# Cosine-similarity attention on one core: four late warm-up dummies behind the first transposes, with new instruction orders

## The chip, the cores and the metric

The kernel runs on one core of a Trainium2 chip. Its engines work in parallel, each through its own queue in program order: TensorE (PE, matmuls and transposes), ScalarE (ACT, exponentials), VectorE (DVE), GpSimd (POOL) and SyncE (SP), which issues nearly all DMAs. They wait for one another on semaphores. The metric is the device time of one launch in microseconds; lower is better.

## What is computed

Queries, keys and values have the shape 8 x 12 x 512 x 64 in float32 (96 heads, 512 rows of 64 numbers), and tau is 0.1.

```
Q_norm = Q / (np.linalg.norm(Q, axis=-1, keepdims=True) + 1e-10)
K_norm = K / (np.linalg.norm(K, axis=-1, keepdims=True) + 1e-10)
scores = np.einsum('bhqd,bhkd->bhqk', Q_norm, K_norm) / tau
weights = np.exp(scores - np.max(scores, axis=-1, keepdims=True))
weights = weights / (np.sum(weights, axis=-1, keepdims=True) + 1e-10)
return np.einsum('bhqk,bhkd->bhqd', weights, V).astype(np.float32)
```

A score is at most 10 in size, so the kernel leaves out the subtraction of the maximum.

## The kernel before

**Tiling.** The work is cut into 48 pairs of heads, s = 0 to 47. For each pair the kernel issues the same small operations, and each has a name of the form `KIND.s.part`:

- `LD.s.0` and `LD.s.1` load queries and keys (256 KB each, line 429, into one of 18 buffers); `LV.s` loads the values (line 432, one of 6).
- `SQ.s` squares both (line 250, mostly on GpSimd). `SSQ.s` adds squares by eight matmuls with an identity (line 268) and `RED.s` (VectorE, line 276) finishes the sums.
- The norms follow. For the first three pairs they are a logarithm and an exponential on ScalarE (`LN.s`, line 282, `EX.s.w`, line 286). For the later ones VectorE iterates in steps `NEW.g.k` (lines 390 to 402) for a group of one or two pairs.
- `SCL.s.0` (queries, VectorE) and `SCL.s.1` (keys, mostly GpSimd) scale the rows into bf16 (line 296).
- `TR.s` transposes the scaled rows on TensorE (line 484) and `EVA.s` copies them from PSUM (VectorE, line 490). Every sixth pair from 9 on transposes its keys by a DMA instead (`XT.s.1`).
- `SCO.s.c`, c = 0 to 3, computes the scores of 128 keys against 512 queries for both heads (two matmuls, line 512), and `EXP.s.c` takes their exponential on ScalarE, 128 x 1024 numbers in one instruction (line 527). The scores lie in PSUM in two halves (`scps`), so TensorE can be at most two chunks ahead of ScalarE.
- `VC.s` converts the values to bf16 (GpSimd, line 532). `PV.s.h.t` multiplies weights and values (four matmuls, line 543); a column of ones in the values gives the sum. `RCP.s` and `NRM.s` (VectorE, lines 557 and 559) divide, and `ST.s` stores (SP).

**The head of the program.** Pair 0 is cut by heads to start sooner. Its loads are four halves. `SQ.0.w.h` (w = 0 queries, 1 keys; h is the head) runs on ScalarE, only `SQ.0.0.1` on GpSimd. `RED.0.w.h` (line 318), `LN.0.h`, `EX.0.h`, `SCL.0.w.h` (line 327), the four transposes of `TR.0.w.h` (line 333), the copy `EVA.0.w.h` (line 338), `SCO.0.h.c` (line 359) and `EXP.0.h.i` (line 364) follow. The transposes need the identity that `one` and `eye` (lines 224 and 225) write on GpSimd; `vone` writes the columns of ones. Pair 1 has its own transposes and copies (lines 301 and 349).

**Dummies.** `warm.0` to `warm.18` are matmuls of 256 columns on a zeroed tile, whose results nothing reads (line 237). `fill.k` are dummies of the same kind that the order puts later. `FILL = (9, 2)` counts those that write the scores' bank and those that write an output bank: in the order of before, fill.0 to fill.7 stand right behind warm.18, fill.8 behind the first two transposes, and fill.9 and fill.10 among the scores of pair 1.

**Order.** Each engine's order is a list written out by hand (`ORDER`). An instruction waits on semaphores for what it needs, and a queue does not pass an instruction that waits. Buffers in PSUM are taken in the order of the list: `x`, `o0` and `o1` are banks that the square sums, the transposes and the outputs share. For TensorE the order of before begins so:

```
warm.15 warm.16 warm.17 warm.18 fill.0 fill.1 fill.2 fill.3 fill.4 fill.5 fill.6 fill.7 TR.0.1.0 TR.0.0.0
fill.8 SCO.0.0.0 SCO.0.0.1 TR.0.1.1 TR.0.0.1 SCO.0.0.2 SCO.0.0.3 SSQ.1 SCO.0.1.0 SCO.0.1.1 SCO.0.1.2 SCO.0.1.3
```

Of the kernel before, what the change touches and what calls it, by code (L numbers as in the profile page):

```python
# [124 lines left out]
def bass_cosine_similarity_attention_kernel(  # L125
# [515 lines left out]
XT = {9: (1,), 15: (1,), 21: (1,), 27: (1,), 33: (1,), 39: (1,), 45: (1,)}  # L641
# [3 lines left out]
WARM = 19  # L645
FILL = (9, 2)
# [5 lines left out]
LOGS = 3  # L652
# [32 lines left out]
        NRM.1 RED.7.0 NEW.2.3 NEW.2.4 NEW.3.0 EVA.4 NEW.2.5 NEW.3.1 NEW.2.6 NEW.3.2 SCL.5.0 NEW.2.7 RCP.2 NRM.2
        RED.9.0 NEW.3.3 NEW.3.4 EVA.5 NEW.3.5 NEW.3.6 NEW.3.7 SCL.6.0 RCP.3 NRM.3 RED.8.0 SCL.7.0 EVA.6 NEW.4.0
        NEW.4.1 RCP.4 NRM.4 NEW.4.2 NEW.4.3 NEW.4.4 EVA.7 NEW.4.5 NEW.4.7 RCP.5 NRM.5 NEW.4.6 RED.10.0 SCL.8.0 SCL.9.0
        EVA.8 EVA.9 RED.11.0 NEW.5.0 NEW.5.1 RCP.6 NRM.6 NEW.5.2 NEW.5.3 NEW.5.4 NEW.5.5 RED.13.0 NEW.5.7 NEW.5.6
        SCL.10.0 RCP.7 NRM.7 RED.12.0 SCL.11.0 EVA.10 NEW.6.0 NEW.6.1 NEW.6.2 EVA.11 NEW.6.3 NEW.6.4 NEW.6.5 NEW.6.6
        SCL.12.0 RED.15.0 RCP.8 NEW.6.7 NRM.8 RED.14.0 NEW.7.0 SCL.13.0 EVA.12 NEW.7.1 NEW.7.2 NEW.7.3 RCP.9 NRM.9  # L690
        NEW.7.4 NEW.7.5 RED.16.0 NEW.7.6 SCL.14.0 EVA.13 NEW.7.7 RCP.10 NRM.10 RED.17.0 EVA.14 SCL.15.0 NEW.8.0
        NEW.8.1 NEW.8.2 EVA.15 NEW.8.3 NEW.8.4 NEW.8.5 RCP.11 NEW.8.6 NRM.11 NEW.8.7 SCL.17.0 RED.18.0 SCL.16.0 RCP.12
        NRM.12 RED.19.0 NEW.9.0 NEW.9.1 NEW.9.2 NEW.9.3 NEW.9.4 EVA.16 RCP.13 NRM.13 RED.20.0 NEW.9.5 EVA.17 NEW.9.7
        NEW.9.6 SCL.18.0 RCP.14 NRM.14 RED.21.0 SCL.19.0 NEW.10.0 EVA.18 EVA.19 NEW.10.1 NEW.10.2 RCP.15 NRM.15
# [15 lines left out]
        RCP.37 NRM.37 NEW.21.3 NEW.21.4 NEW.21.5 RED.44.0 EVA.41 NEW.21.6 SCL.42.0 NEW.21.7 SCL.43.0 RCP.38 NRM.38  # L710
        RED.45.0 EVA.42 NEW.22.0 RCP.39 NRM.39 NEW.22.1 RED.46.0 NEW.22.2 NEW.22.3 EVA.43 NEW.22.4 NEW.22.5 RCP.40
        NRM.40 NEW.22.6 NEW.22.7 RED.47.0 SCL.44.0 RCP.41 NRM.41 SCL.45.0 NEW.23.0 EVA.44 NEW.23.1 NEW.23.2 RCP.42
        NEW.23.3 NRM.42 NEW.23.4 EVA.45 NEW.23.5 NEW.23.6 SCL.46.0 NEW.23.7 RCP.43 NRM.43 EVA.46 SCL.47.0 RCP.44
        NRM.44 EVA.47 RCP.45 NRM.45 RCP.46 NRM.46 RCP.47.0 NRM.47.0 RCP.47.2 RCP.47.1 NRM.47.2 NRM.47.1""",
    "pe": """
# [113 lines left out]
```

## Time and profile before

| | |
|---|---|
| median of three runs | 192.68 us (192.48 to 192.89) |
| profiled execution | 194.2 us, its span 192.4 us |
| ScalarE busy | 182.2 us, 95% |
| TensorE busy | 173.6 us, 90% |
| GpSimd busy | 160.8 us, 84% |
| VectorE busy | 145.1 us, 75% |
| read and written | 37.75 MB and 12.58 MB |

The span runs from the first instruction to the last; the profiled execution's own time has the launch around it. Busy times do not count waiting. In a timeline row the first number is the start in microseconds, the second the time from the first start to the last end of the merged instructions; then come engine, line, operation, what is written and read, and the count. In brackets stands the engine's idle time before the row and what released it. In a row of waits stand the total, the number of times and the longest. Instructions of one engine overlap at their ends by about 0.1 us. In a row of windows the engine's busy time stands behind the length, and behind the count in brackets stand the granted TensorE clock, the DMA share and GB/s.

### The profile page before, as it was taken

To read this page: it belongs to the slowest core of one execution; us is meant where nothing else is said; L and a number is where in the kernel's file an instruction comes from. 1 tells how busy PE (TensorE), PEld (TensorE's weight loads), DVE (VectorE), ACT (ScalarE), POOL (GpSimd) and SP (SyncE) were. 2 spreads that over 40 slices of the span, in tenths; PEclk is the share of its full clock that TensorE was granted. 3 is DMA by queue.
4 is the path that set the end of the run, shared out by engine and by line. 5 is a ranking of instruction groups with operands and counts; after the bars stand their busy time and mean duration, and the time that the engine had idled before them with its cause. 6 is when DMAs were issued, how large, how long until landed. Compare 5 with 4: busy or idle time off the path is not lost.

```text
span 192.4 us, 7254 instructions
## 1 busy us (share of the span) xinstructions
PE 173.6 (90%) x3030; PEld 111.3 (58%) x3030; DVE 145.1 (75%) x451; ACT 182.2 (95%) x209; POOL 160.8 (84%) x147
## 2 busy tenths in 40 slices
PE   7989899998999997898989898999999989997893
PEld 5546566655665665566556565656665656664542
DVE  2789987869878866868868868678689778677523
ACT  5489999999999999999999999999999999999992
POOL 4399599999999997999999999999899997353400
PEclk9999999999999999999999999999999999999998
DMA  5999999479998899989999999999999686513135
GB/s 159 355 349 351 361 342 355 152 241 342 371 334 193 242 345 356 307 214 333 357 332 254 342 298 298 362 237 316 307 385 328 149 259 194 162 27 113 58 114 163
DMA packets 56257, 51.73 MB, mean 269 GB/s; under 512 B 6944, under 2 KB 56224, under 8 KB 56224
## 3 DMA queue, kind: packets, MB, share of 16 engines
q1 hardware_dynamic: 55792, 50.93, 85.0%
q8 instruction: 24, 0.39, 0.8%
q10 hardware_dynamic: 432, 0.33, 0.5%
q14 instruction: 9, 0.07, 0.1%
HBM read 37.75 MB, written 12.58 MB: 262 GB/s over the span
## 4 chain that ended last, share of the span: by engine, by line
ACT 56%; POOL 19%; PE 13%; DMA 4%; DVE 3%; issue 2%; SPq 1%; DVEq 0%; POOLq 0%
ACT et L527 53%; POOL sq L250 11%; POOL qn L296 6%; DMA qk<-in_K_dram 4%; PE scps L512 3%; PE bps L543 3%; PE scps L237 3%; POOL vb L532 2%; ACT et L364 1%; PE bps L268 1%; DVE qn L296 1%; PE bps L484 1%; DVE qt L490 1%; SPq L429 1%; PE scps L359 1%
## 5 line engine op out<-in xcount | busy, mean ns | idle before, releaser
L527 ACT ACTIVATE et<-scps 128x1024 bf16<-128x1024 f32 x184 | 169.9, 1053 | 1.3 <-PE scps L512 1.1
L250 POOL TENSOR_TENSOR sq<-qk 128x1024 bf16<-128x1024 f32 (+2 forms) x48 | 87.9, 1842 | 5.3 <-DMA qk<-in_Q_dram 5.0
L512 PE MATMUL scps<-qt 64*128 64x512 bf16 x376 | 73.7, 385 | 8.1 <-ACT et L527 7.2
L543 PE MATMUL bps<-vb,et 128*128 128x65 bf16 x1504 | 67.4, 194 | 1.9 <-DVE ob L559 0.6
L543 PEld LDWEIGHTS bps<-vb,et 128*128 128x128 bf16 x1504 | 53.0, 98 | 25.0 <-issue 15.3
L296 POOL TENSOR_TENSOR qn<-qk,rk 128x512 bf16<-128x512 f32 x44 | 45.3, 1044 | 12.1 <-DVE rk L398 5.9
L490 DVE COPY qt<-bps 128x1024 bf16<-128x1024 bf16 (+1 forms) x46 | 29.8, 649 | 12.7 <-PE bps L484 12.4
L296 DVE TENSOR_TENSOR qn<-qk,nps 128x512 bf16<-128x512 f32 x50 | 33.5, 682 | 1.1 <-ACT nps L286 0.6
L559 DVE TENSOR_TENSOR ob<-bps,rd 128x512 f32<-128x512 f32 x47 | 32.5, 691 | 1.5 <-DMA out_dram<-ob 0.2
L512 PEld LDWEIGHTS scps<-qt 64*128 64x128 bf16 x376 | 18.3, 93 | 24.7 <-ACT et L527 12.9
L532 POOL TENSOR_SCALAR vb<-vf 128x512 bf16<-128x512 f32 x48 | 29.5, 628 | 1.0 <-DMA vf<-in_V_dram 1.0
L268 PE MATMUL bps<-sq,ident 128*128 128x128 bf16 x376 | 29.1, 220 | 0.3 <-POOL sq L250 0.3
L268 PEld LDWEIGHTS bps<-sq,ident 128*128 128x128 bf16 x376 | 21.2, 98 | 10.2 <-issue 7.1
L557 DVE RECIPROCAL rd<-bps 128x8 f32<-128x8 f32 x47 | 9.7, 207 | 19.1 <-PE bps L543 18.8
L484 PE MATMUL bps<-ident,qn 64*128 64x64 bf16 x680 | 17.8, 191 | 3.4 <-DVE nps L276 0.8
L484 PEld LDWEIGHTS bps<-ident,qn 64*128 64x128 bf16 x680 | 13.7, 95 | 11.3 <-DVE nps L276 2.6
L276 DVE TENSOR_REDUCE nps<-bps 128x16 f32<-128x128 f32 x45 | 13.2, 294 | 1.8 <-PE bps L268 1.8
L394 DVE SCALAR_TENSOR_TENSOR nps<-nps,ys 128x32 f32<-128x32 f32 (+1 forms) x48 | 9.3, 194 | 1.0
L390 DVE TENSOR_TENSOR nps<-nps,ys 128x32 f32<-128x32 f32 (+1 forms) x48 | 9.2, 192 | 0.9
L237 PE MATMUL scps<-warm_in 128*128 128x256 bf16 x28 | 6.1, 409 | 1.1 <-DVE warm_in L232 1.1
L237 PEld LDWEIGHTS scps<-warm_in 128*128 128x128 bf16 x28 | 4.0, 146 | 2.7 <-DVE warm_in L232 1.1
L364 ACT ACTIVATE et<-scps 128x1024 bf16<-128x1024 f32 (+1 forms) x5 | 4.0, 846 | 1.4 <-PE scps L359 1.4
(45 smaller groups left out, 46.0 us busy)
## 6 DMA issues: line engine op xcount, KB each, us to landing
vf<-in_V_dram SPq DMA_DIRECT2D x48, 256.0 KB, 5.9
qk<-in_Q_dram SPq DMA_DIRECT2D x47, 256.0 KB, 5.8
qk<-in_K_dram SPq DMA_DIRECT2D x47, 256.0 KB, 5.7
out_dram<-ob SPq DMA_DIRECT2D x47, 256.0 KB, 4.7
qk<-in_Q_dram SPq DMA_DIRECT2D x2, 128.0 KB, 2.7
qk<-in_K_dram ACTq DMA_DIRECT2D x2, 128.0 KB, 2.9
out_dram<-ob SPq DMA_DIRECT2D x1, 128.0 KB, 2.5
qt<-qn SPq DMA_TRANSPOSE x7, 3.6
```

The lines of the kernel that those rows point to most:

```text
L237: P.add(key, "pe", needs, lambda e: e.matmul(out=bank[:, 0:256], lhsT=warm_in[:, 0:128], rhs=warm_in[:, :], start=True, stop=True))
L250: emit = lambda e: e.tensor_tensor(out=b, in0=a, in1=a, op=ALU.mult)
L268: last = e.matmul(out=ps[:, 0:128], lhsT=ident[:, :], rhs=sq[s % R_SQ][:, :, 8 * k : 8 * k + 8], start=(k == 0), stop=(k == 7))
L276: lambda e: e.tensor_reduce(out=dst(None), in_=ps[:, 0:128].rearrange("p (w g e) -> p w g e", w=2, e=8), axis=AX.X, op=ALU.add))
L296: lambda e: e.tensor_tensor(out=o, in0=x, in1=r, op=ALU.mult))
L484: last = e.transpose(t_ps[:, k, b, :], qn[s % R_QN][ks, b // NT, b % NT].rearrange("p h d -> p (h d)"), ident[ks, ks])
L490: lambda e, lo=lo, hi=hi: e.tensor_copy(out=qt[iqt][:, :].rearrange("p w t (k x) -> p k (w t) x", k=2)[:, :, lo:hi], in_=t_ps[:, :, lo:hi]))
L512: last = e.matmul(out=sc_ps[:, 2 * b + k, :], lhsT=qt[iqt][64 * h : 64 * h + 64, 1, n, :], rhs=qt[iqt][64 * h : 64 * h + 64, 0, :, :], sta ...
L527: lambda e, c=c, b=b: e.activation(out=et[iet][:, c, :, :], in_=sc_ps[:, 2 * b : 2 * b + 2, :], func=ACT.Exp, scale=scale, bias=bias))
L532: lambda e: e.tensor_scalar(out=vb[:, iq, :, :, 0:DIM].rearrange("p c h d -> p h c d"), in0=vf[iv][:, :, :].rearrange("p h (c d) -> p h c ...
L543: last = e.matmul(out=o_ps[:, h, 65 * t : 65 * t + 65], lhsT=et[iet][:, c, h, 128 * t : 128 * t + 128], rhs=vb[:, iq, c, h, :], start=(c = ...
L559: lambda e: e.tensor_tensor(out=ob[io][:, :], in0=grid[:, :, :, 0:DIM], in1=rd[io][:, :].unsqueeze(3).to_broadcast([128, 2, NT, DIM]), op= ...
```

## The change

Four dummies stand behind the transposes of the first head instead of the late dummies of before. `FILL` becomes `(4, 0)`, so there are 23 dummies in all instead of 30, and the first `fill` names the transposes of the first head as what it follows. fill.9 and fill.10 go with the rest.

All five orders are written anew. What an instruction does and on which engine it runs stay the same. The differences near the start, and some later ones:

- TensorE: TR.0.1.0 and TR.0.0.0 follow warm.18 directly, then the four fills. The four scores SCO.0.0.0 to SCO.0.0.3 stand in a row ahead of TR.0.1.1 and TR.0.0.1. From pair 2 on, transposes, square sums, scores and outputs are interleaved a little differently, by one to three instructions as a rule.
- ScalarE: SQ.0.0.0 ahead of SQ.0.1.0; LN.2 and EX.2 ahead of EXP.0.1.1 instead of behind it.
- VectorE: RED.0.1.1 ahead of the first scalings and RED.0.0.1 behind them; SCL.3.0 ahead of SCL.3.1; many steps NEW at other places.
- GpSimd: SQ.0.0.1 ahead of `one`, `eye` and `vone`. Many VC move by up to several places, and some SQ: SQ.28.0 now stands ahead of SQ.26.0.
- SyncE: loads and stores in another order; among the first, ST.1 stands ahead of LV.5 and LD.10, and LD.11, LD.13 and LD.14 come later.

```diff
@@ kernel @@
         dummy(("fill", k), sc_ps[:, 3] if low else o_ps[:, 0],
-              [("fill", k - 1) if k else ("warm", WARM - 1), "wz" if low else ("RED", 2, 0) if LOGS > 2 else ("EVA", 0, 1, 1)])
+              [*([("fill", k - 1)] if k else [("TR", 0, w, 0) for w in range(2)]), "wz" if low else ("RED", 2, 0) if LOGS > 2 else ("EVA", 0, 1, 1)])
...
-FILL = (9, 2)
+FILL = (4, 0)
@@ ORDER "pe" @@
-        warm.15 warm.16 warm.17 warm.18 fill.0 fill.1 fill.2 fill.3 fill.4 fill.5 fill.6 fill.7 TR.0.1.0 TR.0.0.0
-        fill.8 SCO.0.0.0 SCO.0.0.1 TR.0.1.1 TR.0.0.1 SCO.0.0.2 SCO.0.0.3 SSQ.1 SCO.0.1.0 SCO.0.1.1 SCO.0.1.2 SCO.0.1.3
-        SSQ.2 TR.1.0 TR.1.1 SCO.1.0 SSQ.3 SCO.1.1 fill.9 TR.2 SCO.1.2 fill.10 PV.0.0.0 SCO.1.3 PV.0.0.1 PV.0.0.2 SSQ.4
...
+        warm.15 warm.16 warm.17 warm.18 TR.0.1.0 TR.0.0.0 fill.0 fill.1 fill.2 fill.3 SCO.0.0.0 SCO.0.0.1 SCO.0.0.2
+        SCO.0.0.3 TR.0.1.1 TR.0.0.1 SSQ.1 SCO.0.1.0 SCO.0.1.1 SCO.0.1.2 SCO.0.1.3 SSQ.2 TR.1.0 TR.1.1 SCO.1.0 SSQ.3
+        SCO.1.1 PV.0.0.0 SCO.1.2 TR.2 PV.0.0.1 PV.0.0.2 PV.0.0.3 SCO.1.3 PV.0.1.0 PV.0.1.1 SCO.2.0 SSQ.4 PV.0.1.2
...
@@ ORDER "act" @@
-        LD.0.1.0 LD.0.1.1 table SQ.0.1.0 SQ.0.0.0 SQ.0.1.1 LN.0.0 EX.0.0 LN.0.1 EX.0.1 SQ.1.0 EXP.0.0.0 EXP.0.0.1
-        EXP.0.0.2 LN.1 EX.1.1 EX.1.0 EXP.0.1.0 EXP.0.1.1 LN.2 EX.2.0 EX.2.1 EXP.1.0 EXP.1.1 EXP.1.2 EXP.1.3 EXP.2.0
+        LD.0.1.0 LD.0.1.1 table SQ.0.0.0 SQ.0.1.0 SQ.0.1.1 LN.0.0 EX.0.0 LN.0.1 EX.0.1 SQ.1.0 EXP.0.0.0 EXP.0.0.1
+        EXP.0.0.2 LN.1 EX.1.0 EX.1.1 EXP.0.1.0 LN.2 EX.2.1 EX.2.0 EXP.0.1.1 EXP.1.0 EXP.1.1 EXP.1.2 EXP.1.3 EXP.2.0
@@ ORDER "dve" @@
-        wz RED.0.1.0 RED.0.0.0 RED.0.0.1 SCL.0.1.0 SCL.0.0.0 RED.0.1.1 EVA.0.1.0 EVA.0.0.0 SCL.0.1.1 SCL.0.0.1 SQ.1.1
+        wz RED.0.0.0 RED.0.1.0 RED.0.1.1 SCL.0.1.0 SCL.0.0.0 RED.0.0.1 EVA.0.1.0 EVA.0.0.0 SCL.0.0.1 SCL.0.1.1 SQ.1.1
...
@@ ORDER "pool" @@
-        one eye vone SQ.0.0.1 SQ.2.0 SQ.2.1 SQ.3.0 VC.0 SQ.4.0 SQ.5.0 VC.1 SQ.6.0 SQ.7.0 SCL.4.1 VC.2 SQ.9.0 SCL.5.1
-        VC.3 SQ.8.0 SCL.6.1 VC.4 VC.5 SCL.7.1 SQ.10.0 VC.6 VC.8 SCL.9.1 SCL.8.1 SQ.11.0 SQ.13.0 VC.7 SQ.12.0 SCL.10.1
...
+        SQ.0.0.1 one eye vone SQ.2.0 SQ.2.1 SQ.3.0 VC.0 SQ.4.0 SQ.5.0 VC.1 SQ.6.0 SQ.7.0 SCL.4.1 VC.2 SQ.9.0 SCL.5.1
+        VC.3 SQ.8.0 SCL.6.1 VC.4 VC.6 VC.5 VC.7 SCL.7.1 SQ.10.0 SCL.8.1 SCL.9.1 SQ.11.0 SQ.13.0 SQ.12.0 VC.8 SCL.10.1
...
+        SCL.21.1 SCL.20.1 VC.18 SQ.24.0 SQ.25.0 VC.20 VC.19 SCL.22.1 SQ.28.0 SQ.26.0 SCL.23.1 SQ.27.0 VC.22 VC.21
...
@@ ORDER "sp" @@
-        LD.6.1 LD.7.0 LD.7.1 LD.9.0 LV.2 LD.9.1 LV.4 LV.3 LV.6 LD.8.0 LD.8.1 LD.11.0 ST.0 LV.5 LD.10.0 LD.10.1 LD.14.0
...
+        LD.6.0 LD.7.0 LD.7.1 LD.9.0 LV.2 LD.9.1 LV.3 LD.8.0 LV.6 LV.4 LD.8.1 ST.1 LV.5 LV.7 LD.10.0 LD.10.1 ST.2
...
```

More of the change, by code (lines that the diff above doesn't have):

```diff
@@ L685 @@
[L685 to L694, printed above, removed]
@@ L710 @@
[L710 to L714, printed above, removed]
+        NEW.0.2 NEW.0.3 NEW.0.4 EVA.2 NEW.0.5 NEW.0.6 NEW.0.7 SCL.3.0 SCL.3.1 RED.4.0 RCP.0 NEW.1.0 NRM.0 RED.5.0
```

199 lines of the change are left out of this document (106 added, 93 removed).

## The prediction

> **What bounds the kernel now.** I read the page first (busy times, the 40 slices, the chain), then ScalarE's waits, then its timeline, and only then the head of the program engine by engine.
>
> ```profile
> PE 173.6 (90%) x3030; PEld 111.3 (58%) x3030; DVE 145.1 (75%) x451; ACT 182.2 (95%) x209; POOL 160.8 (84%) x147
> ACT  5489999999999999999999999999999999999992
> ACT 56%; POOL 19%; PE 13%; DMA 4%; DVE 3%; issue 2%; SPq 1%; DVEq 0%; POOLq 0%
> ```
>
> ScalarE works 182.2 of 192.4 us, and its busy share falls under nine tenths only in the first three slices and the last. That work is the same after the change, so the time can move only by ScalarE's idle time. The group of its waits in the steady part, then its timeline rows that begin after a wait:
>
> ```profile
> ACT et L527 <- PE scps L512: 1.1, 3, 0.5
> 8.51 1.08 ACT L364 ACTIVATE et<-scps 128x512 bf16<-128x512 f32 x2 [1.21 <-PE scps L359]
> 9.82 1.02 ACT L364 ACTIVATE et<-scps 128x1024 bf16<-128x1024 f32 x1 [0.23 <-PE scps L359]
> 13.98 8.40 ACT L527 ACTIVATE et<-scps 128x1024 bf16<-128x1024 f32 x9 [0.46 <-PE scps L512]
> 22.73 51.69 ACT L527 ACTIVATE et<-scps 128x1024 bf16<-128x1024 f32 x56 [0.34 <-PE scps L512]
> 74.75 109.95 ACT L527 ACTIVATE et<-scps 128x1024 bf16<-128x1024 f32 x119 [0.33 <-PE scps L512]
> ```
>
> TensorE makes ScalarE wait 1.21 + 0.23 + 0.46 = 1.90 us in the head of the program, and 0.34 + 0.33 us in the 170 us that follow. So the prize lies in the first 14 us, and the danger in a long middle that is already almost without holes.
>
> **The head, row by row.** These rows carry the sum.
>
> ```profile
> 1.06 0.29 POOL L225 TENSOR_SCALAR_AFFINE_SELECT ident<-ones 128x128 bf16<-128x128 bf16 x1
> 1.10 5.80 PE L237 MATMUL scps<-warm_in 128*128 128x256 bf16 x27 [1.10 <-DVE warm_in L232]
> 4.09 0.61 POOL L250 TENSOR_TENSOR sq<-qk 128x256 bf16<-128x256 f32 x1 [1.94 <-DMA qk<-in_Q_dram]
> 5.55 0.41 DVE L327 TENSOR_TENSOR qn<-qk,bps 128x256 bf16<-128x256 f32 x1
> 6.68 0.61 ACT L248 ACTIVATE sq<-qk 128x512 bf16<-128x512 f32 x1
> 6.83 0.63 PE L333 MATMUL bps<-ident,qn 128*64 128x128 bf16 x8
> 6.97 0.50 PE L333 MATMUL bps<-ident,qn 128*64 128x128 bf16 x6
> 7.25 0.22 PE L333 MATMUL bps<-ident,qn 128*64 128x128 bf16 x1
> 7.28 0.75 DVE L338 COPY qt<-bps 64x512 bf16<-64x512 bf16 x2 [0.99 <-PE bps L333]
> 7.40 0.28 PE L237 MATMUL scps<-warm_in 128*128 128x256 bf16 x1
> 8.09 0.60 PE L359 MATMUL scps<-qt 64*128 64x512 bf16 x2 [0.40 <-DVE qt L338]
> 9.35 0.77 DVE L338 COPY qt<-bps 64x512 bf16<-64x512 bf16 x2
> 10.38 0.29 DVE L276 TENSOR_REDUCE xs<-bps 128x16 f32<-128x128 f32 x1 [0.26 <-PE bps L268]
> 10.98 0.28 ACT L286 ACTIVATE nps<-xl 128x8 f32<-128x8 f32 x2
> 11.29 1.28 DVE L296 TENSOR_TENSOR qn<-qk,nps 128x512 bf16<-128x512 f32 x2 [0.62 <-ACT nps L286]
> ```
>
> The second scaling (SCL.0.0.0, line 327) ends at 5.96, yet its transposes start at 6.83: 27 dummies, 19 warm and 8 fill, stand ahead of them. They follow each other every 0.21 us ((5.80 - 0.28) / 26), while the last six transposes follow every 0.055 us ((0.50 - 0.22) / 5). A dummy streams 256 columns and a transpose 128, so the dummies ran at half the rate, and the full rate came at about 6.9.
>
> **Fill dummies, and TR.0 ahead of them.** The 19 warm dummies end at about 1.10 + 19 x 0.21 + 0.2 = 5.3. TR.0.1.0 then waits for SCL.0.1.0, about 5.65, still at the half rate: 4 x 0.11 = 0.43 us. TR.0.0.0 follows from 6.09 to 6.52, with its result some 0.18 later, at 6.70. Of the four fills behind it, two pass at 0.21 and, with the full rate at 6.9, two at 0.11: TensorE is free at 7.16. The two copies (line 338) take 0.41 each; the second runs from 6.72 to 7.11. SCO.0.0.0 starts at 7.16 instead of 8.09. EXP.0.0.0 follows as before 0.42 later, at 7.58 instead of 8.51; ScalarE is free from 7.29.
>
> **The four first scores ahead of TR.0.x.1.** Back to back at 0.22 (line 359's pair takes 0.60, one 0.38) the last is done at 8.2, so EXP.0.0.2 no longer waits for transposes: 7.58 + 1.06 = 8.64 to 9.66, where it ended at 10.84. The second head's transposes start at 8.04, behind all four, and hide beside these exponentials. VectorE, which had stood 0.99 us idle, finishes its copies at about 9.25 (10.12 before) and RED.1.0 at 9.5 (10.67).
>
> **LN.2 and EX.2 ahead of EXP.0.1.1.** After EXP.0.0.2, LN.1 and EX.1 take 0.5 as they do now, and EXP.0.1.0 runs from 10.05 to 11.05. VectorE scales pair 1 from 10.1 to 11.35, then reduces pair 2 until 11.6. LN.2 now stands first in ScalarE's queue and waits for that: 0.55 us idle, with EXP.0.1.1 queued behind it. Then 0.5 for LN.2 and EX.2, and EXP.0.1.1 from 12.1 to 13.05. Pair 1's transposes and copies are done by 12.3, its SCO.1.0 by 12.75, so EXP.1.0 starts at 13.05 without a wait instead of at 13.98: **-0.93 us**. In return SCL.2.1 starts at about 12.3, before ScalarE's first row of line 527, and VectorE's queue for pairs 2 to 4 is a microsecond ahead.
>
> **fill.9 and fill.10.** Each holds TensorE about 0.11 us (256 columns at the full rate). They stand between 14.7 and 16.0, where TensorE feeds ScalarE closely; the next late thing is the score before EXP.3.1, the 0.34 us wait at 22.73, still behind SSQ.6 and four PV. Bounds 0 and -0.34; I take **-0.1**, half of the two dummies, since only part of that stretch is TensorE's own queue.
>
> **First orders on POOL, ScalarE and VectorE.** SQ.0.0.1 ahead of the constants leaves it waiting for its load until 4.09 as now; the identity (0.29 us, after a shorter memset) comes some 0.5 us after its end at 4.70, so near 5.25, before 5.65. ScalarE's first three squares change places, but the last still waits for the second half of K. Cost nothing; if the identity were 0.5 us later it would delay TR.0.1.0.
>
> **SP.** ST.1 now stands ahead of LV.5, LD.10.0 and LD.10.1, and waits for NRM.1:
>
> ```profile
> 20.12 0.66 SPq L432 DMA_DIRECT2D vf<-in_V_dram  x1
> 22.79 0.69 DVE L559 TENSOR_TENSOR ob<-bps,rd 128x512 f32<-128x512 f32 x1
> vf<-in_V_dram SPq DMA_DIRECT2D x48, 256.0 KB, 5.9
> 30.71 1.21 POOL L532 TENSOR_SCALAR vb<-vf 128x512 bf16<-128x512 f32 x2
> 32.89 1.89 POOL L250 TENSOR_TENSOR sq<-qk 128x1024 bf16<-128x1024 f32 x1
> ```
>
> NRM.1 ends at 23.48, so LV.5 issues at 24.2 instead of 20.12 and lands 5.9 later, at 30.1; VC.5, the second at 30.71, takes it at 31.3. LD.10.1 issues fourth, at 26.1, and lands near 32, ahead of SQ.10.0 at 32.89, which itself gets VC.7 ahead of it. If NRM.1 is also a microsecond early, so are they: nothing. Later in the run most loads are issued several microseconds ahead of use in both orders, so I cost SP's order at nothing, with 0.5 us as its upper bound.
>
> **The orders of the middle.** For each instruction I added up the work that stands ahead of it on its engine in both orders. POOL has most at stake; its waits from 22.7 to 138 and the tightest case:
>
> ```profile
> POOL qn L296 <- PE scps L512: 2.1, 1, 2.1
> POOL vb L532 <- DMA vf<-in_V_dram: 1.0, 1, 1.0
> POOL sq L250 <- DMA qk<-in_K_dram: 0.3, 1, 0.3
> 84.34 3.75 POOL L250 TENSOR_TENSOR sq<-qk 128x1024 bf16<-128x1024 f32 x2
> 88.05 2.05 POOL L296 TENSOR_TENSOR qn<-qk,rk 128x512 bf16<-128x512 f32 x2
> 92.07 0.63 POOL L532 TENSOR_SCALAR vb<-vf 128x512 bf16<-128x512 f32 x1
> 92.66 1.89 POOL L250 TENSOR_TENSOR sq<-qk 128x1024 bf16<-128x1024 f32 x1
> 91.43 0.62 PE L268 MATMUL bps<-sq,ident 128*128 128x128 bf16 x8
> 91.98 0.39 PE L512 MATMUL scps<-qt 64*128 64x512 bf16 x2
> ```
>
> After its 2.1 us wait at 22.72 POOL stands still only 1.3 us in 115, so it too must start that stretch earlier for ScalarE's gain to last. It waits there for SCL.4.1's norms, which VectorE, a microsecond ahead, delivers earlier. SQ.26.0, the second square from 84.34 (ends 88.09), now has SQ.28.0 (1.85), VC.20 (0.6) and SCL.22.1 (1.0) ahead of it: 3.45 later, 91.5, against SSQ.26 at 91.43, which in TensorE's queue stands ahead of SCO.22.0. With POOL a microsecond ahead it just fits. The waits left in the middle and the tail (0.33 at 74.75, 0.2 near 187) could go (-0.5), and a new order can open holes; a few of the size seen here, 0.2 to 0.5, make +1.3 an upper bound. I take 0, near what the present order shows.
>
> **Sum.** -0.93 - 0.1 + 0 = -1.0 us. The profiled execution took 194.2 us, its span of 192.4 and 1.8 around it; the sum makes its span 191.4. The unprofiled median, 192.68, lies 1.5 under the profiled execution. I take the difference over: **191.7 us**. Its own range: the head between -0.6 and -1.3, the middle between -0.5 and +0.4, so 190.9 to 192.4.
>
> **Rival 1: the clock stays low (slower).** Unbroken dummies covered 1.10 to 6.9 before the full rate came; after the change TensorE stands idle from 5.3 to 5.65. Those 0.35 us decide. If the rate needs unbroken work as long as the 5.8 us seen, it comes at 5.65 + 5.8 = 11.5. Scores then take 0.43 apart and SCO.0.0.3 is done at 9.26, TR.0.0.1 at 10.1, the copies at 10.5, SSQ.1 at 11.0, EX.1 at 11.7, EX.2 at 13.8, and EXP.1.0 starts near 14.75: +0.77, with -0.1 for the fills 193.4 us. Against it: TensorE still works most of the stretch.
>
> ```profile
> 0.10:3.51 3.41, 2.41 (x12) 1.00 0.45 142
> 3.51:6.92 3.41, 3.41 (x19) 1.00 0.92 297
> ```
>
> The granted clock reads 1.00 in both stretches, so it does not show the half rate; the spacing of the matmuls does. The Trainium skill, "TensorE: Matmul & The Clock Gate", section "The HAM clock gate (the "warmup" mystery)", says that the array gets half its pulses until it has been busy for one window of about 3.4 us, and that windows run on regardless of the kernel's start. By that rule the window that released the clock here began near 3.5; the one before it, 2.41 of 3.41 us busy, did not release it, and no run here shows whether one with a hole of 0.35 us does. If it does not, the next ends at 10.33, and by the same steps the time would be 193.1 us.
>
> **Rival 2: the middle eats the gain (no change).** If POOL's long stretch does not start earlier, SQ.26.0 ends at 91.5 while TensorE, 1.0 us ahead, wants it at 90.4: SSQ.26 blocks SCO.22.0 for 1.1 us and the gain is gone: 192.6. From a POOL lead under 0.3 us on it decides. For it: POOL is nearly without idle time there; against: its start hangs on VectorE, which does move.
>
> **Rival 3: several new holes in the middle.** At the upper bound of +1.3 the sum is 192.68 - 1.03 + 1.3 = 193.0, and with SP's 0.5 as well 193.5.
>
> **How the numbers follow.** A change under 0.2% (0.39 us) can't be told from none, so faster means below 192.3 and slower above 193.07. Forecast 0.56, rival 1 0.18, rival 2 0.14, rival 3 0.12. Of the forecast's cases I put 0.02 within 0.2%, and of rival 3's half, so faster 0.54, same 0.22, slower 0.24. The range from 191.0 to 193.4 leaves out the forecast's best end and the worst mixtures of rivals 1 and 3.
>
> **What would show it.** Right: TR.0.1.0 near 5.65 and SCO.0.0.0 near 7.2; scores of line 359 0.22 apart; ScalarE's wait before EXP.0.0.0 about 0.3 in place of 1.21; a new wait of about 0.5 before LN.2; the first row of line 527 near 13.05; POOL's SCL.4.1 near 21.6; at most 0.5 us of waits of line 527 behind it. Wrong: scores 0.43 apart (rival 1); a wait of ScalarE for the scores behind SSQ.26 near 91 (rival 2); more than three waits of line 527 (rival 3).

## The result and the profile after

The changed kernel takes 192.22 us (median of 22 executions); the kernel before 192.83 us (22 executions). The ratio is 0.9967, 95% interval 0.9952 to 0.9982. In a second comparison (below) it is 0.9983, 0.9961 to 1.0005. So the change gains some 0.2 to 0.3%, about 0.3 to 0.6 us, where 1.0 us was forecast; the second interval alone would not exclude that it gains nothing. The profiled execution of the changed kernel took 192.64 us, its span 190.9 us.

From the page of the changed kernel: busy times, ScalarE's 40 slices, the chain by engine, and the group of the exponentials:

```profile
PE 172.5 (90%) x3023; PEld 110.4 (58%) x3023; DVE 145.2 (76%) x451; ACT 181.9 (95%) x209; POOL 160.2 (84%) x147
ACT  4589999999999999999999999999999999999992
ACT 78%; DVE 6%; PE 6%; POOL 5%; DMA 3%; issue 1%; SPq 0%; DVEq 0%
L527 ACT ACTIVATE et<-scps 128x1024 bf16<-128x1024 f32 x184 | 169.7, 1069 | 0.4
```

ScalarE does the same work and is still the bound. The idle time in front of line 527 fell to 0.4 us in all (the last number of its row); the same row of the kernel before has 1.3. ScalarE's timeline of the changed kernel, the rows that matter:

```profile
7.58 0.63 ACT L248 ACTIVATE sq<-qk 128x512 bf16<-128x512 f32 x1 [0.86 <-DMA qk<-in_Q_dram]
8.12 1.98 ACT L364 ACTIVATE et<-scps 128x512 bf16<-128x512 f32 x3
12.16 0.22 ACT L282 ACTIVATE xl<-xs 128x16 f32<-128x16 f32 x1 [0.61 <-DVE xs L276]
13.52 170.03 ACT L527 ACTIVATE et<-scps 128x1024 bf16<-128x1024 f32 x184
186.51 1.08 ACT L523 ACTIVATE et<-scps 128x512 bf16<-128x512 f32 x2 [0.21 <-PE scps L512]
```

The 184 exponentials of line 527 now merge into one row: no single wait among them was long enough to split it. TensorE in the same head:

```profile
1.10 3.93 PE L237 MATMUL scps<-warm_in 128*128 128x256 bf16 x19 [1.10 <-DVE warm_in L232]
5.67 0.74 PE L333 MATMUL bps<-ident,qn 128*64 128x128 bf16 x8 [0.63 <-DVE qn L327]
6.98 1.03 PE L359 MATMUL scps<-qt 64*128 64x512 bf16 x4
```

The transposes start at 5.67 and the four scores follow each other at the full rate: 4 in 1.03 us, (1.03 - 0.38) / 3 = 0.22 apart. But the load of pair 1's queries (LD.1.0) landed at 7.56; ScalarE's square of them stands ahead of EXP.0.0.0 and waited 0.86 us.

The two profiled executions first compared differ by 1.46 us of span, in three stretches: EXP.1.0 starts 0.46 earlier (13.98 to 13.52), from there to EXP.47.3.0 0.69 less (173.68 to 172.99), and from EXP.47.3.0 to the end 0.30 less (4.70 to 4.40). The experiments show that this subtraction misleads: most of it is the spread between executions of one kernel (two profiles of the kernel before have spans of 192.4 and 190.2).

### The profile page after: what moved, and what is told of

The parts are those of the page before. It is cut to its first block, busy times and chain, and to the rows that moved or that the text cites. A ratio compares the mean times of both kernels' runs of the same rounds, so it can differ in the third digit from the quotient of the medians.

```text
span 190.9 us, 7237 instructions
## 1 busy us (share of the span) xinstructions
PE 172.5 (90%) x3023; PEld 110.4 (58%) x3023; DVE 145.2 (76%) x451; ACT 181.9 (95%) x209; POOL 160.2 (84%) x147
## 4 chain that ended last, share of the span: by engine, by line
ACT 78%; DVE 6%; PE 6%; POOL 5%; DMA 3%; issue 1%; SPq 0%; DVEq 0%
ACT et L527 76%; DMA qk<-in_Q_dram 3%; POOL sq L250 3%; PE scps L512 2%; DVE qn L296 2%; PE bps L543 2%; POOL qn L296 1%; ACT et L364 1%; DVE qt L490 1%; PE bps L268 1%; POOL vb L532 1%; ACT et L523 1%; DVE nps L276 1%; PE bps L484 0%; SPq L315 0%
## 5 line engine op out<-in xcount | busy, mean ns | idle before, releaser
L543 PE MATMUL bps<-vb,et 128*128 128x65 bf16 x1504 | 69.4, 194 | 1.0 <-issue 0.3
L543 PEld LDWEIGHTS bps<-vb,et 128*128 128x128 bf16 x1504 | 53.6, 98 | 26.7 <-issue 18.4
L237 PE MATMUL scps<-warm_in 128*128 128x256 bf16 x23 | 4.5, 377 | 1.1 <-DVE warm_in L232 1.1
L402 DVE TENSOR_SCALAR ys<-nps 128x32 int32<-128x32 int32 (+1 forms) x24 | 4.4, 183 | 0.4
L398 DVE SCALAR_TENSOR_TENSOR nps<-nps,ys 128x16 f32<-128x16 f32 (+1 forms) x25 | 4.3, 175 | 0.4
```

What stands on the lines that cost most here:

```text
L543: last = e.matmul(out=o_ps[:, h, 65 * t : 65 * t + 65], lhsT=et[iet][:, c, h, 128 * t : 128 * t + 128], rhs=vb[:, iq, c, h, :], start=(c = ...
```

## Experiments

A table of the profiles with 19 warm-up dummies comes first, since each experiment gives a value to each column. "Full rate" is the time of the change of clock that the trace records for TensorE; "middle" is the time from the start of EXP.1.0 to that of EXP.47.3.0, "tail" from there to the end of the span. All in us.

| kernel | late dummies | full rate | TR.0.1.0 | LD.1.0 landed | EXP.1.0 | middle | tail |
|---|---|---|---|---|---|---|---|
| before | old | 6.62 | 6.83 | 6.20 | 13.98 | 173.68 | 4.70 |
| before_again | old | 4.00 | 5.74 | 5.34 | 12.95 | 172.69 | 4.55 |
| tail_alone | old | 6.14 | 6.59 | 6.07 | 13.74 | 172.67 | 4.64 |
| before_loads | old | 4.12 | 5.68 | 6.38 | 12.90 | 172.75 | 4.66 |
| orders_alone | old | 4.63 | 5.86 | 5.63 | 13.37 | 174.23 | 4.38 |
| dummies_alone | new | 5.42 | 5.75 | 6.58 | 12.96 | 173.45 | 4.97 |
| dummies_loads | new | 5.81 | 5.76 | 7.61 | 13.45 | 173.51 | 4.81 |
| head_alone | new | 6.40 | 5.54 | 7.51 | 13.50 | 172.82 | 4.90 |
| after | new | 4.58 | 5.67 | 7.56 | 13.52 | 172.99 | 4.40 |
| after_again | new | 4.47 | 5.74 | 5.96 | 13.04 | 173.70 | 4.37 |
| after_old_tail | new | 4.85 | 5.58 | 6.03 | 12.88 | 172.66 | 4.47 |
| ln_behind | new | 6.95 | 5.63 | 5.44 | 13.15 | 172.81 | 4.35 |
| after_loads | new | 4.62 | 5.53 | 7.03 | 13.01 | 172.97 | 4.39 |

### The change taken apart: dummies, orders, head

dummies_alone is the kernel before with the new late dummies and nothing else:

```diff
-FILL = (9, 2)
+FILL = (4, 0)
-        ... warm.18 fill.0 fill.1 fill.2 fill.3 fill.4 fill.5 fill.6 fill.7 TR.0.1.0 TR.0.0.0 fill.8 SCO.0.0.0 ...
+        ... warm.18 TR.0.1.0 TR.0.0.0 fill.0 fill.1 fill.2 fill.3 SCO.0.0.0 ...
-        ... SCO.1.1 fill.9 TR.2 SCO.1.2 fill.10 PV.0.0.0 ...
+        ... SCO.1.1 TR.2 SCO.1.2 PV.0.0.0 ...
```

> The orders of before, with only the dummies changed: no fill ahead of the first transposes, four behind them, none later. Theory A (the dummies held up the head): SCO.0.0.0 starts near 7.0 instead of 8.09, EXP.1.0 near 13.0 to 13.4 instead of 13.98, ratio to before about 0.995 to 0.997. Theory B (the gain comes from the new orders of the middle): EXP.1.0 may come earlier, but the waits of line 527 behind it take it back, ratio 0.999 or more. Theory C (fewer dummies keep the clock low in some executions): scores of line 359 0.43 apart and a ratio above 1.000.

Measured: 193.08 us, ratio to the kernel before 1.0026 (1.0007 to 1.0045): slower, so theory A's ratio missed. Yet its head is as good as theory A hoped, EXP.1.0 at 12.96. The time went later. ScalarE, GpSimd and TensorE of dummies_alone near pair 18:

```profile
77.47 2.98 ACT L527 ACTIVATE et<-scps 128x1024 bf16<-128x1024 f32 x3 [0.42 <-PE scps L512]
73.07 1.21 POOL L532 TENSOR_SCALAR vb<-vf 128x512 bf16<-128x512 f32 x2 [1.01 <-DMA vf<-in_V_dram]
74.53 3.74 POOL L250 TENSOR_TENSOR sq<-qk 128x1024 bf16<-128x1024 f32 x2 [0.25 <-DMA qk<-in_K_dram]
76.48 0.62 PE L268 MATMUL bps<-sq,ident 128*128 128x128 bf16 x8 [0.64 <-POOL sq L250]
```

A late load of values (LV.18) and a late load of keys (LD.22.1) stop GpSimd; its square is late, the square sums SSQ.22 wait for it in TensorE's queue, and the scores SCO.18.1 stand behind them. It is the mechanism of the prediction's rival 2, but at SSQ.22 instead of SSQ.26, and set off by loads. LV.18 is issued at 64.90 and lands at 73.00; in before_again (below) it is issued at 64.87 and lands at 72.20.

orders_alone is the reverse: all new orders, with the eleven old late dummies at their old places (fill.9 and fill.10 side by side ahead of PV.0.0.0).

```diff
-FILL = (4, 0)
+FILL = (9, 2)
-        ... warm.18 TR.0.1.0 TR.0.0.0 fill.0 fill.1 fill.2 fill.3 SCO.0.0.0 ...
+        ... warm.18 fill.0 fill.1 fill.2 fill.3 fill.4 fill.5 fill.6 fill.7 TR.0.1.0 TR.0.0.0 fill.8 SCO.0.0.0 ...
-        SCO.1.1 PV.0.0.0 ...
+        SCO.1.1 fill.9 fill.10 PV.0.0.0 ...
```

> The orders of after, with the eleven late dummies of before at the places they had. Theory A: TR.0.1.0 starts where 27 dummies end, 6.0 to 6.9 by when the full rate comes, EXP.1.0 at 13.5 to 14.0, ratio 0.998 to 1.001. Theory B: ratio 0.996 to 0.998, the same as the whole change. Theory C: ratio below that of the whole change.

Measured: 192.78 us, ratio 1.0011 (0.9990 to 1.0033): theory B's ratio missed, theory A's met within the noise. Here the full rate came early, at 4.63, so TR.0.1.0 starts at 5.86 and the old dummies cost little. The new orders have a place of the same kind as SSQ.22. ScalarE and GpSimd of orders_alone:

```profile
55.04 3.77 ACT L527 ACTIVATE et<-scps 128x1024 bf16<-128x1024 f32 x4 [0.80 <-PE scps L512]
52.11 1.89 POOL L250 TENSOR_TENSOR sq<-qk 128x1024 bf16<-128x1024 f32 x1 [1.68 <-DMA qk<-in_K_dram]
```

Here SQ.16.0 waits 1.68 us for LD.16.1, which SyncE issues at 44.76, behind LV.14, and which lands 7.3 us later, at 52.04; in the profile of after it took 5.6 us and landed at 49.59.

head_alone has the new dummies and the new orders of TensorE, ScalarE, VectorE and GpSimd as far as SCO.1.1, EXP.0.1.1, SCL.2 and `vone`; the rest of every order is that of before.

```diff
-        ... TR.0.0.0 fill.8 SCO.0.0.0 SCO.0.0.1 TR.0.1.1 TR.0.0.1 SCO.0.0.2 SCO.0.0.3 SSQ.1 ...
+        ... TR.0.0.0 fill.0 fill.1 fill.2 fill.3 SCO.0.0.0 SCO.0.0.1 SCO.0.0.2 SCO.0.0.3 TR.0.1.1 TR.0.0.1 SSQ.1 ...
-        EXP.0.0.2 LN.1 EX.1.1 EX.1.0 EXP.0.1.0 EXP.0.1.1 LN.2 EX.2.0 EX.2.1 EXP.1.0 ...
+        EXP.0.0.2 LN.1 EX.1.0 EX.1.1 EXP.0.1.0 LN.2 EX.2.1 EX.2.0 EXP.0.1.1 EXP.1.0 ...
```

> The dummies and the orders of after up to the scores of pair 1 (VectorE up to EVA, SCL and RED.3.0 ahead of NEW.0.0), then the orders of before. Theory A: EXP.1.0 as in after (13.0 to 13.5), ratio 0.995 to 0.997. Theory B: EXP.1.0 as in after, but waits of line 527 of 0.8 us or more behind it, as in before, ratio 0.998 to 1.000.

Measured: 192.67 us, ratio 1.0009 (0.9993 to 1.0025). Its rows of TensorE and ScalarE tell two things:

```profile
5.54 1.03 PE L333 MATMUL bps<-ident,qn 128*64 128x128 bf16 x8 [0.20 <-DVE qn L327]
7.08 1.03 PE L359 MATMUL scps<-qt 64*128 64x512 bf16 x4
7.53 0.63 ACT L248 ACTIVATE sq<-qk 128x512 bf16<-128x512 f32 x1 [0.93 <-DMA qk<-in_Q_dram]
```

The eight transposes take 1.03 us, the low rate, and the four scores 1.03 us, the full rate, although TensorE had stood idle just ahead of the transposes; so this hole did not keep the clock low. And the load of pair 1 came at 7.51, which put EXP.1.0 at 13.50 as in the first profile after. Of the two theories neither is met: the ratio is not theory A's, and the one wait of line 527 over 0.15 us is 0.22, not theory B's 0.8 or more.

### The same kernels once more

after_again is the changed kernel itself, before_again the kernel before itself; neither has an edit.

> The changed kernel once more. If the late landing of pair 1's queries in its first profile (ScalarE waited 0.86 us for them before SQ.1.0 at 7.58) belongs to the change, SQ.1.0 starts near 7.6 again and EXP.1.0 near 13.5. If it is chance, SQ.1.0 starts near 6.7 and EXP.1.0 near 13.05. Ratio 0.995 to 0.998 either way.

Measured: 192.35 us, ratio 0.9983 (0.9961 to 1.0005).

> The kernel before once more, for its profile. Theory D (the eight dummies ahead of the transposes cost what is left of the half rate when they run, so their price goes with the moment the full rate comes): TR.0.1.0 starts at 5.9 if the full rate comes by 4.9 us, at 6.8 if it comes near 6.9; EXP.1.0 then starts between 13.0 and 14.0 in step with it. If the head of before is the same in every execution instead, TR.0.1.0 starts at 6.83 again. ScalarE's waits in the middle: 0.3 before EXP.3.1 again if they belong to the order, and one of 0.3 to 0.5 somewhere between 70 and 100.

Measured in one execution: 191.93 us, its span 190.2. TensorE and ScalarE of before_again, to be set beside the same rows of the prediction:

```profile
1.10 4.52 PE L237 MATMUL scps<-warm_in 128*128 128x256 bf16 x27 [1.10 <-DVE warm_in L232]
5.74 0.74 PE L333 MATMUL bps<-ident,qn 128*64 128x128 bf16 x8
12.95 8.40 ACT L527 ACTIVATE et<-scps 128x1024 bf16<-128x1024 f32 x9 [0.46 <-PE scps L512]
21.69 59.01 ACT L527 ACTIVATE et<-scps 128x1024 bf16<-128x1024 f32 x64 [0.34 <-PE scps L512]
```

This settles the head. The same 27 dummies took 4.52 us where they had taken 5.80: the full rate came at 4.00 instead of 6.62, so TensorE had worked them off by the time the scaled rows were there, and the old dummies cost nothing. The wait of 0.33 us at pair 17 is missing too (one row runs over it). The profile on which the prediction rested was near the worst that the old dummies can do: at the low rate throughout, 27 of them would end at about 6.9 (1.10 + 27 x 0.21), and there TR.0.1.0 started at 6.83.

By the table, with the old dummies TR.0.1.0 follows the full rate: 5.68 to 5.86 when it came by 4.63, 6.59 and 6.83 when it came at 6.14 and 6.62. With the new ones it is 5.53 to 5.76 whatever the moment, even at 6.95. What the new dummies give is that head's independence of the moment, not 0.93 us each time. Over the profiles EXP.1.0 starts at 13.39 on average with the old dummies (five) and at 13.19 with the new (eight). LD.1.0 landed past 7.5 in three of the eight; dummies move no data, so I take that for chance, though no run tests it. Without these three the average is 13.01, a gain of 0.38 us.

The Trainium skill, "TensorE: Matmul & The Clock Gate", section "The HAM clock gate (the "warmup" mystery)", says that the windows which set the clock run free of the kernel's start, so that the moment differs between runs. The runs agree on that: the moment lies between 4.00 and 6.95, and the rate's end follows it by 184.32 us in most profiles and by 187.73 in others, 3.41 more; 184.32 is 54 times 3.413.

### Is the hole in the warm-up near a cliff?

warm10 is the changed kernel with ten warm-up dummies instead of 19.

```diff
-WARM = 19
+WARM = 10
-        ... warm.9 warm.10 ... warm.18 TR.0.1.0 ...
+        ... warm.9 TR.0.1.0 ...
```

> The kernel after with 10 in place of 19 warm-up dummies at the start, so that TensorE stands idle from about 3.2 to 5.65 us. If work before the first transposes is what brings TensorE's full rate, the rate comes after the first heads' scores: the scores of head 0 lie 0.43 us apart in place of 0.22, EXP.0.0.0 starts at 8 us or later, ratio to the kernel after 1.003 or more (0.999 to 1.002 to the kernel before). If the new late dummies and transposes bring it as well, EXP.1.0 starts by 13.2 and the ratio to the kernel before is 0.996 to 0.998.

Measured: 197.3 us, ratio to the kernel before 1.0234 (1.0193 to 1.0274). TensorE and ScalarE of warm10:

```profile
1.10 2.32 PE L237 MATMUL scps<-warm_in 128*128 128x256 bf16 x10 [1.10 <-DVE warm_in L232]
5.80 1.06 PE L333 MATMUL bps<-ident,qn 128*64 128x128 bf16 x8 [2.38 <-DVE qn L327]
7.76 1.89 PE L359 MATMUL scps<-qt 64*128 64x512 bf16 x4
8.40 1.08 ACT L364 ACTIVATE et<-scps 128x512 bf16<-128x512 f32 x2 [0.99 <-PE scps L359]
16.41 1.02 ACT L527 ACTIVATE et<-scps 128x1024 bf16<-128x1024 f32 x1 [0.19 <-PE scps L512]
17.91 1.94 ACT L527 ACTIVATE et<-scps 128x1024 bf16<-128x1024 f32 x2 [0.48 <-PE scps L512]
20.53 5.77 ACT L527 ACTIVATE et<-scps 128x1024 bf16<-128x1024 f32 x6 [0.68 <-PE scps L512]
```

The scores lie 0.42 apart, as the theory of the early work had it, but the price was far under-estimated: the full rate came only at 21.0. EXP.1.0 starts 3.4 us later than in after_again, and 0.48 and 0.68 us of waits for scores follow. So the mechanism of rival 1 exists and costs some 5 us. In these profiles the change stays on the safe side of it: where the hole of the new dummies lay ahead of the full rate, it was 0.20 us (head_alone), 0.30 us (ln_behind) and 0.42 us (dummies_loads), and the rate came at 6.40, 6.95 and 5.81. TensorE of dummies_loads:

```profile
5.76 0.74 PE L333 MATMUL bps<-ident,qn 128*64 128x128 bf16 x8 [0.42 <-DVE qn L327]
```

Nothing between that and 2.38 us was tried, and warm10 also has nine dummies fewer, so the length of the hole is not tested by itself. The windows of warm10 show that busy time alone does not bring the rate:

```profile
7.50:10.90 3.40, 3.40 (x18) 1.00 1.06 357
10.90:14.30 3.40, 3.40 (x21) 1.00 1.10 354
17.70:21.00 3.30, 3.30 (x48) 1.00 1.10 348
```

Two stretches in which TensorE never stood still left it at the low rate; a later one, as full by the row, ended with the full rate. The first has mostly scores and transposes of tiles 64*128 and 128*64, half of the dummies' 128*128 each; the last has outputs of 128*128 and scores that overlap in pairs. That the gate counts used parts of the array is a guess, and the kept traces fit it better than busy time. For an estimate, weigh each matmul by its columns, 0.21 us per 256 at the low rate, and by its tile's share of 128*128. Then, in the fourteen profiles, the stretches of 3.41 us that end with the change are filled to 0.69 to 1.00, and those before them to 0.72 at most; by busy time it is 0.85 to 1.00 and up to 1.00. By the weights the two ranges just cross, by busy time they overlap widely. The weights were chosen afterwards, and no run tests them.

The same section of the Trainium skill has the full rate come after one busy window of about 3.4 us; by that warm10 should have had it at 10.8 at the latest, where the first window that begins behind 5.80 ends (21.0 less three times 3.41), and it did not come.

### LN.2 behind EXP.0.1.1 again

```diff
-        EXP.0.0.2 LN.1 EX.1.0 EX.1.1 EXP.0.1.0 LN.2 EX.2.1 EX.2.0 EXP.0.1.1 EXP.1.0 ...
+        EXP.0.0.2 LN.1 EX.1.0 EX.1.1 EXP.0.1.0 EXP.0.1.1 LN.2 EX.2.1 EX.2.0 EXP.1.0 ...
```

> The changed kernel with LN.2 and EX.2 behind EXP.0.1.1 on ScalarE, as in before. If the wait of 0.61 us before LN.2 is a price of the new order: no such wait, EXP.1.0 starts 0.2 us earlier relative to EXP.0.1.0 than in after (2.8 instead of 2.98), ratio 0.996 to 0.998. If it only moves the wait: 0.2 to 0.5 us before EXP.1.0 or EXP.2.0, ratio as in after.

Measured: 192.10 us, ratio 0.9977 (0.9957 to 0.9997). ScalarE of ln_behind:

```profile
10.36 1.92 ACT L364 ACTIVATE et<-scps 128x1024 bf16<-128x1024 f32 x2
13.15 1.94 ACT L527 ACTIVATE et<-scps 128x1024 bf16<-128x1024 f32 x2 [0.46 <-PE scps L512]
```

TensorE of ln_behind in the head:

```profile
5.63 1.06 PE L333 MATMUL bps<-ident,qn 128*64 128x128 bf16 x8 [0.30 <-DVE qn L327]
7.31 1.03 PE L359 MATMUL scps<-qt 64*128 64x512 bf16 x4
```

Here the full rate came latest of all, at 6.95, behind a hole of 0.30 us, and the scores start only 0.25 us later than in after_again. The wait of 0.61 us ahead of LN.2 is gone, and one of 0.46 us ahead of EXP.1.0 takes its place, the one that the kernel before has. From EXP.0.1.0 to EXP.1.0 it is 2.79 us, as the first theory has it, in after_again 2.98: LN.2 ahead costs 0.19 us there. In the whole time ln_behind and the changed kernel can't be told apart.

### The stores at the end

tail_alone is the kernel before with two stores moved; after_old_tail undoes that move in the changed kernel.

```diff
-        ... ST.41 ST.40 ST.43 ST.45 ST.42 ST.44 ST.46 ST.47.0 ST.47.1
+        ... ST.41 ST.40 ST.42 ST.44 ST.43 ST.45 ST.46 ST.47.0 ST.47.1
```

> The kernel before with one change in SP's queue: ST.42 and ST.44 ahead of ST.43 and ST.45 instead of behind them. Theory E (in before three stores go out together with the last ones and hold them up; the new order of SP sends them early, a gain that the prediction costed at nothing): from the start of the last exponentials to the end of the span 4.4 us instead of 4.7 to 5.0, ratio 0.997 to 0.999. Without theory E: 4.7 or more, ratio 1.000.

Measured: 192.59 us, ratio 0.9994 (0.9974 to 1.0015); the tail is 4.64, between the two forecasts.

> The changed kernel with SP's last stores in the old order (ST.43, ST.45, ST.42, ST.44). Theory E: from the start of the last exponentials to the end of the span 4.7 to 5.0 us instead of 4.4, and a ratio of 0.999 to 1.001, the gain of the whole change mostly gone. If the gain is the head's alone: ratio 0.997 to 0.998 still.

Measured: 192.33 us, ratio 0.9985 (0.9964 to 1.0005). Its tail is 4.47, again between. No effect of this move alone on the time can be told. But the tail column is steady: 4.35 to 4.40 in the five profiles with all of the new orders and no move there, 4.55 to 4.97 in the kernels that end in the old ones. From EXP.47.3.0 to the last issue it is 2.2 us in nine of the fourteen profiles and 2.3 to 2.8 in the others, the four with the longest tails among these; the landing differs too. The issues of the last 128 KB store, in before_again and then in after_again (the last number is the time from issue to landing):

```profile
out_dram<-ob SPq DMA_DIRECT2D x1, 128.0 KB, 2.3
```

```profile
out_dram<-ob SPq DMA_DIRECT2D x1, 128.0 KB, 1.7
```

In the old order three stores are issued 2.6 to 1.7 us ahead of EXP.47.3.0. In before_again the last of them lands at 186.95, 0.88 us after ST.46 was issued, and ST.46 takes 2.8 us to land; in after_again the last store ahead of ST.46 has landed by then, and ST.46 takes 2.2. Moving two of them changes the tail of single profiles by about 0.1 us (4.64 and 4.47), so this explains the difference in part. warm10, with the new order, has 4.95, so other things count too; this stays open.

### The late loads of the middle

Theory F: the holes at pairs 17 and 18 of the old order, and at 12 and 13 of the new, are loads that SyncE issues too late for some executions. before_loads and dummies_loads issue LV.18 and LD.22.1 (and LD.22.0) earlier, in the kernel before and in dummies_alone; after_loads does the like for pair 16 in the changed kernel.

```diff
-        LD.21.0 LD.23.0 LD.27.0 LD.22.0 ST.7 LD.28.0 LV.18 LD.28.1 LD.22.1
+        LD.21.0 LD.22.0 LD.22.1 LV.18 LD.23.0 LD.27.0 ST.7 LD.28.0 LD.28.1
```

```diff
-        LD.20.0 LD.14.0 LD.14.1 LV.10 ST.0 LD.16.0 LV.9 LV.11 LV.14 LD.16.1
+        LD.20.0 LD.14.0 LD.14.1 LD.16.0 LD.16.1 LV.10 ST.0 LV.9 LV.11 LV.14
```

> The kernel before with the new late dummies alone, and in SyncE's order LV.18 and LD.22.1 issued three to four places earlier. Theory F (the wait of dummies_alone before EXP.18.1, 0.42 and 0.35 us, comes from these two loads landing late, at 72 to 75.6 us): VectorE's and GpSimd's steps of pair 18 and head 22 find their data, no ScalarE wait over 0.1 at EXP.17.1 to EXP.18.1, ratio 0.996 to 0.999 in place of 1.0026. Rival (the wait belongs to the order of the compute engines): the wait stays, ratio 1.001 or more.

Measured: 193.0 us, ratio 1.0022 (0.9997 to 1.0047): missed. The wait at pair 18 is gone, as the theory says, but another one, unlike any before, stands in this profile. TensorE and ScalarE of dummies_loads:

```profile
29.83 0.39 PE L512 MATMUL scps<-qt 64*128 64x512 bf16 x2 [0.74 <-ACT et L527]
30.27 1.94 ACT L527 ACTIVATE et<-scps 128x1024 bf16<-128x1024 f32 x2 [0.54 <-PE scps L512]
```

SCO.5.1 needs the half of the score bank that EXP.4.3 freed at 28.81, and starts 1.0 us after that. The row names ScalarE, but the exponential that ended just before, EXP.5.0, read the other half. Nothing in the trace explains it.

> The kernel before with the same move of LV.18 and LD.22.1 and nothing else. Theory F: the 0.33 us before EXP.17.1 goes, ratio 0.997 to 0.999. Rival (the wait is not the loads', or it is only rarely there): 1.000 within 0.001.

Measured: 192.35 us, ratio 0.9980 (0.9959 to 1.0001): as theory F expects, though the interval just reaches 1 and before_again lacks the wait at pair 17 without the move. ScalarE of before_loads runs over pairs 17 and 18 in one row, and GpSimd converts the two values there (VC.18 and VC.16) without a wait:

```profile
69.49 11.18 ACT L527 ACTIVATE et<-scps 128x1024 bf16<-128x1024 f32 x12
71.99 1.22 POOL L532 TENSOR_SCALAR vb<-vf 128x512 bf16<-128x512 f32 x2
```

> The kernel after with LD.16.0 and LD.16.1 issued ahead of LV.10, ST.0, LV.9, LV.11 and LV.14. Theory F applied to the new order: GpSimd has no wait before SQ.16.0 (1.2 and 1.7 us in two of the runs with this order), no ScalarE wait at EXP.12.0 to EXP.13.0, ratio 0.995 to 0.998. Rival (the loads that are moved back are needed as early, or the wait is only rarely there): 0.998 or above.

Measured: 192.2 us, ratio 0.9976 (0.9955 to 0.9997). GpSimd squares pair 16 without a wait in after_loads (first row); in after_again, which needs the load at the same place, it waits:

```profile
50.58 1.89 POOL L250 TENSOR_TENSOR sq<-qk 128x1024 bf16<-128x1024 f32 x1
```

```profile
51.38 1.89 POOL L250 TENSOR_TENSOR sq<-qk 128x1024 bf16<-128x1024 f32 x1 [1.22 <-DMA qk<-in_K_dram]
58.34 7.63 ACT L527 ACTIVATE et<-scps 128x1024 bf16<-128x1024 f32 x8 [0.26 <-PE scps L512]
```

Locally theory F holds for pair 18 in dummies_alone and for pair 16 in the new orders. The wait of 0.33 us ahead of EXP.17.1 in before is something else. TensorE of before ahead of it, then GpSimd of before and of before_again at VC.18 and VC.16:

```profile
74.03 0.35 PE L543 MATMUL bps<-vb,et 128*128 128x65 bf16 x6 [0.27 <-issue]
74.13 1.21 POOL L532 TENSOR_SCALAR vb<-vf 128x512 bf16<-128x512 f32 x2 [1.01 <-DMA vf<-in_V_dram]
```

```profile
72.27 1.21 POOL L532 TENSOR_SCALAR vb<-vf 128x512 bf16<-128x512 f32 x2 [0.23 <-DMA vf<-in_V_dram]
```

TensorE stood 0.27 us between two of the four matmuls of PV.15.0.1, with nothing to wait for that the profile shows, and the scores stand behind it. VC.18 and VC.16 are needed only behind those scores, and dummies_alone, whose GpSimd waits the same 1.01 us for LV.18, has no wait at pair 17. The profile of after has one such stall as well, 0.26 us at 52.03; its cause is open. As a gain in time theory F is not proven: after_loads can't be told from the changed kernel (0.9967 and 0.9983), and the hole that it closes stood in two of the six profiles with that order of loads (warm10 counted). Why the new dummies in the old orders are slower than the kernel before (1.0026, and 1.0022 with the loads moved) stays open: their profiles show the load, a late LD.1.0, an unexplained stall and a tail of 4.8 to 5.0, each in one or two executions.

## Why the prediction was right, and where it was off

The forecast, faster, came true, and the time lies within the range; the size was 0.3 to 0.6 us instead of 1.0.

- **Fill dummies, and TR.0 ahead of them.** The path itself was right, though the full rate read at 6.9 was at 6.62 by the trace's record: TR.0.1.0 at 5.65 forecast, 5.53 to 5.76 measured; SCO.0.0.0 at 7.16, measured 6.84 to 7.31.
- **Four scores in a row, LN.2.** EXP.0.0.2 was forecast at 8.64, in after_again 8.45; the new wait ahead of LN.2 at 0.55, measured 0.61; EXP.1.0 at 13.05, in after_again 13.04. In the profile of after it is 13.52 since LD.1.0 landed at 7.56. That load was taken to be in time as in the profile before, and no bound was put on it.
- **The mis-sized term is the -0.93.** The 13.05 was compared with 13.98 of one execution, and the difference was then taken over to the median. But the 1.5 us by which that execution lay above its median were in part this very wait for the clock. Over the profiles the term is 0.20 us on average, 0.38 without the late loads, and between 0 and about 1.0 in a single execution. The head's own range, -0.6 to -1.3, does not hold either average.
- **fill.9 and fill.10, -0.1.** In the old orders (dummies_alone against before_again) taking them away moved no exponential of the first 17 pairs by more than 0.02 us: nothing, not 0.1. The wait ahead of EXP.3.1 fell from 0.34 to 0.11 only with the new orders.
- **First orders, SP, middle, 0.** As a sum right: the middle takes 172.66 to 173.70 us in the changed kernel's two profiles and the two with its middle untouched (after_old_tail, ln_behind), 172.67 to 173.68 in the kernel before and tail_alone. SP's order was given 0.5 us at most, and the late LD.16.1 is followed by a wait of ScalarE of 0.26 us in after_again, in orders_alone of 0.80 and 0.26: the bound was too low.
- **Tail, 0.** Here 0.2 to 0.3 us were gained that the prediction did not have, mostly in the landing of the last stores. So about half of what was gained has a source that the prediction put at nothing, and that the time came out on the forecast side is in part luck.
- **Rival 1** did not happen: with the new dummies the rate came between 4.47 and 6.95, and holes of 0.20, 0.30 and 0.42 us ahead of it did no harm; the last is longer than the 0.35 us on which the rival was to turn. warm10 shows that the mechanism is real with a hole of 2.38 us and ten dummies, and that its price of 0.7 us over the time before was far too low.
- **Rival 2** did not happen at SSQ.26; its mechanism did, at other places and from late loads. (By its own terms, 192.68 - 1.03 + 1.1, its time is 192.75, not 192.6.) **Rival 3** is what orders_alone shows, with waits of 0.80, 0.26 and 0.14 us ahead of EXP.12.0, EXP.13.0 and EXP.19.3.

## What to carry to other kernels

Before a wait in one profile is counted as the prize, profile the same kernel a second time: here the 1.2 us between the scaled keys of the first head (ready at 5.63) and their transposes (6.83) were the draw of one execution; in another of the same kernel they were gone (5.68 and 5.74). A change that makes a stretch independent of such a draw is worth the mean of the draw, not its worst. And a queue of loads issued just in time turns a gain in the head into a new wait elsewhere, so the parts of a change must be tried together as well as alone: dummies and orders alone each gave nothing (1.0026 and 1.0011), together 0.9967. Which part of the 0.3 to 0.6 us each gives is therefore not shown; the profiles' averages put 0.2 to 0.4 in the head and 0.2 to 0.3 in the tail.

## What the hardware showed that was not expected

- The moment of the full TensorE rate differs between executions of one kernel from 4.00 to 6.62 us (kernel before), and nothing else need differ: dummies_alone and before_again, which have it at 5.42 and 4.00, start every exponential within 0.02 us of each other up to EXP.18.0.
- An idle 0.20 us of TensorE ahead of 5.54 left the rate to come at 6.40, and one of 0.42 us ahead of 5.76 at 5.81. After an idle 2.38 us it came at 21.0, behind stretches that the profile shows as fully busy.
- The granted clock reads 1.00 in windows of half rate ahead of the recorded change, so there the spacing of matmuls must be read instead.
- The same load, LD.1.0, issued at 1.70 or 1.71 us in every profile, landed between 5.34 and 7.61 us. LV.18, in the old order of loads, took 5.8 to 8.2 us from issue to landing (tail_alone and before).
